# Decoder layer in split float32: one 512-column product in place of two of 256 columns

## The chip, the cores and the metric

One core of a Trainium2 chip runs the whole kernel. The metric is the device time of one execution in microseconds; of several executions the median is taken.

## What is computed

One hybrid decoder layer on 256 tokens of width 2048, in float32:

```python
h = rms_norm(x, attn_norm_g)
proj = h @ w_in                                   # 2048 x 4448
y_rwkv = rwkv7_mixer(token_shift(proj[...]), ...) # 16 heads of 64, a recurrence over the tokens
y_mla = mla_mixer(c_q, c_kv, k_pe, positions, ...)# 8 heads, latents of 512, causal softmax
x = x + concat(y_rwkv, y_mla) @ w_out
h = rms_norm(x, ffn_norm_g)
x = x + (silu(conv3(h @ w_gate)) * (h @ w_up)) @ w_down   # d_ff = 5632
return rms_norm(x, final_norm_g)
```

## The kernel before

All large products are made in three parts. A float32 factor is split into a high part (rounded to the matmul's input type) and a low part (the rest), and the product is hi·hi + hi·lo + lo·hi, all added in PSUM. Weights come from HBM in pieces of 128 x 1024 floats. `piece` (L118) loads one on SP's queue, ScalarE (ACT) rounds it into `hi` (L126) and VectorE (DVE) subtracts to get `lo` (L127). `raw`, `hi` and `lo` have three buffers each, so the cast for a piece needs the buffer that the piece three before it has left.

Two helpers issue the products. `prod_b` (L149) holds a weight tile of 128 x 128 in the array and streams the activations of all 256 tokens; the result is feature-major, 128 features x 256 tokens. For each tile of the contraction (a "k tile") it issues three matmuls of 256 columns: high weights with high activations (L160), high weights with low activations (L161), low weights with high activations (L162). Every matmul has a weight load of its own. `prod_a` (L165) holds activations and streams 512 columns of weights, also three matmuls per k tile and token block (L172 to L174); the change does not touch it.

`prod_b` serves three users:

- `in_tile` (L179): the 35 column tiles of the input projection, 16 k tiles each. The first five (three in `acc0`, two in `kacc`) are made while the kernel starts, before the row norms `rsB` are known; the first two go by L154 with `by_pass=True`: all four hi·hi, then all four hi·lo, then the lo·hi of a group of k tiles.
- `up_b` (L761): 10 pieces of the latents' up projection, two results of 4 k tiles each.
- the gated MLP (L914 to L935): 44 column tiles, gate and up, 16 k tiles each, in two blocks of 24 and 20; each block is followed by its part of the down projection, which is `prod_a`.

So there are 35·16 + 10·2·4 + 44·2·16 = 2048 k tiles in `prod_b`. A result occupies half of a PSUM bank tile of 128 x 512 (`mm`, three buffers). It is evicted by one VectorE multiplication with a per-token scale: `h` (L363, in `shifted`), `kraw` (L414), `cr` (L727), `dsts` (L767), `gt` (L924), `up` (L931).

The activations' two parts lie in separate tiles: `xhi`, `xlo` (two each, 8 k tiles per tile) for the input, `chi`, `clo` for the latents, `zhi`, `zlo` for the MLP. They are filled by a ScalarE operation and a VectorE subtraction each (L136, L137; L734, L735; L880, L881).

In time the stages are: start (to some 41 us), decay, keys, receptance, values with the triangular solves on VectorE beside them (to some 250 us), the recurrence over four chunks with the latents and `up_b` as matmuls between its steps (to some 349 us), attention and output projection (to some 490 us), MLP block 0, down, block 1, down. The order on each engine is not the program's: the tile framework places instructions by a simulated timeline (`schedule_with_timeline_sim=True`), SP's queue at the start by hand. Within one accumulator the matmuls stay in the program's order.

Of the kernel before, what the change touches and what calls it, by code (L numbers as in the profile page):

```python
# [17 lines left out]
P = 128  # L18
# [36 lines left out]
def hybrid_layer(ctx: ExitStack, tc: tile.TileContext, a: dict, out: bass.AP):  # L55
# [24 lines left out]

    def t1(n, w=T, dt=F32):
        return sb.tile([P, 260], dt, tag="t1", name=nm(n), bufs=NT1)[:, :w]
# [20 lines left out]
    xhi = [a8("xhi") for _ in range(2)]  # L103
    xlo = [a8("xlo") for _ in range(2)]
# [25 lines left out]
    def xsplit(g):  # L130
        raw = s4(n="xraw").rearrange("p (k t) -> p k t", k=4)
        nc.sync.dma_start(raw, xT[:, g * 4:(g + 1) * 4, :])
        for j in range(4):
            k = g * 4 + j
            h = xhi[k // 8][:, k % 8, :]
            S.activation(h, raw[:, j, :], AF.Copy, scale=vv("ag", k))  # L136
            V.scalar_tensor_tensor(xlo[k // 8][:, k % 8, :], raw[:, j, :], vv("ag", k),  # L137
                                   h.bitcast(F32), ALU.mult, ALU.subtract)
        return raw
# [36 lines left out]
    x_hi = lambda k: xhi[k // 8][:, k % 8, :]  # L176
    x_lo = lambda k: xlo[k // 8][:, k % 8, :]

    def in_tile(i, pf=mm):  # L179
        acc = pf()[:, :T]  # L180
        for h in range(2):
            prod_b(acc, piece(a["win"][i, h]), x_hi, x_lo, h * 8, 8, h == 0, h == 1)
            if h == 0:
                flush()
        return acc

    def rsqrt(src, scale, eps, w, eng=None, part=None):
        """1/sqrt(src * scale + eps) on [P, w]: integer seed and three Newton steps on -y."""
        e = eng or nc.gpsimd
        m, y, t = st("rm", w), st("ry", w), st("rt", w)  # L190
        if part is None:
            e.tensor_scalar(m, src, 0.5 * scale, 0.5 * eps, ALU.mult, ALU.add)
        else:
            e.tensor_scalar(part, part, 0.5 * scale, 0.5 * eps, ALU.mult, ALU.add)
# [24 lines left out]
    # sums over features of squares, token-major, accumulated over feature tiles  # L219
# [64 lines left out]
    # sigmoid(x) = 0.5 tanh(x/2) + 0.5  # L284
# [9 lines left out]
    acc0 = [mm()[:, :T], mm()[:, :T], at()[:, :T]]  # L294
# [11 lines left out]
    with tc.manual_schedule(engines={mybir.EngineType.SP}):  # L306
        for g in range(4):
            xsplit(g)
            if g == 0:
                nc.scalar.dma_start(cst, a["cst"])  # L310
            if g == 2:
                rope_tables()
            if g % 2 == 0:
                for i in range(2):
                    pcs[i, g // 2] = piece(a["win"][wt0[i], g // 2])
            for i in range(2):
                hl = tuple(u[:, (g % 2) * 512:(g % 2 + 1) * 512] for u in pcs[i, g // 2])
                prod_b(acc0[i], hl, x_hi, x_lo, g * 4, 4, g == 0, g == 3, True)
        for h in range(2):
            prod_b(acc0[2], piece(a["win"][26, h]), x_hi, x_lo, h * 8, 8, h == 0, h == 1)  # L320
# [93 lines left out]
    V.tensor_tensor(kraw[0:64], acc[0:64], rsB[0:64], ALU.mult)  # L414
# [36 lines left out]
    # squared inverse key norms: token-major [t, (p, w, h)], and per problem  # L451
# [266 lines left out]
    chi, clo, rrs, rrB = [], [], [], []  # L718

    def latent(x, gname, post):  # L720
        h_, l_ = s4(F32R, "chi"), s4(F32R, "clo")
        h_, l_ = (u.rearrange("p (k t) -> p k t", k=4) for u in (h_, l_))
        ssum = t2("css")
        for j in range(4):
            acc = in_tile(27 + x * 4 + j)
            cr = t2("cr")
            V.tensor_tensor(cr, acc, rsB, ALU.mult)  # L727
# [6 lines left out]
            S.activation(h_[:, j, :], cr, AF.Copy, scale=vv(gname, j))  # L734
            V.scalar_tensor_tensor(l_[:, j, :], cr, vv(gname, j), h_[:, j, :].bitcast(F32), ALU.mult, ALU.subtract)  # L735
# [11 lines left out]
        chi.append(h_)  # L747
        clo.append(l_)
# [12 lines left out]
    def up_b(src, i, x, dsts):  # L761
        pcs = piece(src[i])
        for j in range(2):
            acc = mm()[:, :T]
            prod_b(acc, (pcs[0][:, j * 512:(j + 1) * 512], pcs[1][:, j * 512:(j + 1) * 512]),
                   lambda k: chi[x][:, k, :], lambda k: clo[x][:, k, :], 0, 4, True, True)
            V.tensor_tensor(dsts[j], acc, rrB[x], ALU.mult)  # L767
# [24 lines left out]
    for cc in range(2):  # L792
        accs = [mm() for _ in range(2)]
        for i in range(2):
            prod_a(accs, piece(a["wuv"][cc, i]), lambda k: chi[1][:, k, :], lambda k: clo[1][:, k, :],
# [60 lines left out]
    zhi, zlo = zip(*((a8("zhi"), a8("zlo")) for _ in range(2)))  # L856
    for half in (0, 1):
        for c in range(4):
# [8 lines left out]
            if half == 1:  # L867
# [3 lines left out]
                for j in range(2):  # L871
# [5 lines left out]
                    for k in range(2):  # L877
                        kt = c * 4 + j * 2 + k
                        hv = zhi[kt // 8][:, kt % 8, :]
                        S.activation(hv, pt[:, k, :], AF.Copy, scale=vv("fg", kt))  # L880
                        V.scalar_tensor_tensor(zlo[kt // 8][:, kt % 8, :], pt[:, k, :], vv("fg", kt),  # L881
# [8 lines left out]
    z_hi = lambda k: zhi[k // 8][:, k % 8, :]  # L890
    z_lo = lambda k: zlo[k // 8][:, k % 8, :]
# [19 lines left out]
    for blk, nf in enumerate((24, 20)):  # L911
        hh = [s4(F32R, "hh").rearrange("p (k t) -> p k t", k=4) for _ in range(nf // 4)]
        hl = [s4(F32R, "hl").rearrange("p (k t) -> p k t", k=4) for _ in range(nf // 4)]
        for fi in range(nf):  # L914
            f = f0 + fi
            accs = []
            for gu in range(2):
                acc = mm()[:, :T]
                for h in range(2):
                    prod_b(acc, piece(a["wgu"][f, gu, h]), z_hi, z_lo, h * 8, 8, h == 0, h == 1)  # L920
# [3 lines left out]
            V.tensor_tensor(gt[:, 2:258], accs[0], rs2B, ALU.mult)  # L924
# [6 lines left out]
            V.tensor_tensor(up, accs[1], rs2B, ALU.mult)  # L931
# [117 lines left out]
```

## Time and profile before

| | |
|---|---|
| time, three runs | median 1246.21 us (1246.03 to 1254.26) |
| span of the profiled execution | 1248.2 us |
| TensorE (PE) busy | 1227.7 us, 98% |
| weight loads (PEld) | 1129.7 us, 91% |
| VectorE (DVE) busy | 786.2 us, 63% |
| ScalarE (ACT) busy | 563.9 us, 45% |
| granted clock of TensorE, mean | 0.992 |

The profiled execution is one execution, and its span is 2.0 us above the median of the timed runs. Matmuls are pipelined: one's duration in the trace (some 283 ns) overlaps the next, so a matmul's price in a dense stretch is the distance from one start to the next, not its duration.

### The profile page before, as it was taken

The page shows a single profiled execution, that of the slowest core. Times are in us where ns is not written, and L with a number is a line of the kernel's source. Part 1 is how long each engine was busy: PE and PEld are TensorE (multiplying, and loading weights), DVE is VectorE, ACT ScalarE, POOL GpSimd, SP SyncE. Part 2 cuts the span into 40 slices and gives each one's busy share as a digit, 9 for nine tenths or more (in the row PEclk, how much of TensorE's full clock was granted, in tenths as well). Part 3 has the DMA queues.
Part 4 walks back from the last instruction along what each step waited for, and adds up shares of the span by engine and source line. Part 5 has one row for each costly group of instructions (what it writes and reads, how often), then busy time and mean ns, then how long its engine had stood idle before and what let it go on. Part 6 is the DMA issues. An engine that isn't in the chain of part 4 may idle for free.

```text
span 1248.2 us, 22026 instructions
## 1 busy us (share of the span) xinstructions
PE 1227.7 (98%) x8945; PEld 1129.7 (91%) x8945; DVE 786.2 (63%) x1195; ACT 563.9 (45%) x787; POOL 52.3 (4%) x196
## 2 busy tenths in 40 slices
PE   7999999999999999999999999999999999999996
PEld 6889999998867888999999999888899999998885
DVE  6886658755667566666666665545466666665563
ACT  6773245422234445544444444333344444444451
POOL 3300000101110001000000000000000000000000
PEclk9999999998999999999999999999999999999999
DMA  8634445733323455565555555656655555566662
GB/s 305 197 120 141 124 147 178 201 114 114 111 85 128 159 178 176 176 183 183 186 185 181 181 183 186 193 188 191 201 187 186 181 180 184 184 218 205 213 205 87
DMA packets 70773, 216.04 MB, mean 173 GB/s; under 512 B 17360, under 2 KB 17616, under 8 KB 70672
## 3 DMA queue, kind: packets, MB, share of 16 engines
q1 hardware_dynamic: 69520, 211.84, 53.5%
q10 hardware_dynamic: 768, 2.05, 0.5%
q8 instruction: 70, 1.15, 0.4%
q0 software_dynamic: 384, 0.75, 0.2%
q14 instruction: 31, 0.25, 0.1%
HBM read 210.48 MB, written 3.41 MB: 171 GB/s over the span
## 4 chain that ended last, share of the span: by engine, by line
PE 97%; DMA 1%; DVE 1%; issue 0%; ACT 0%; ACTq 0%; POOL 0%; DVEq 0%; POOLq 0%
PE mm L160 19%; PE mm L162 19%; PE mm L161 19%; PE mm L172 9%; PE mm L173 9%; PE mm L174 9%; PE pg L504 1%; PE px L636 1%; PE px L645 1%; PE psc L816 1%; DMA raw<-in_win 1%; PE px L632 1%; PE py L662 1%; PE psc L814 1%; PE mm L154 0%; DMA rp<-in_pos 0%
## 5 line engine op out<-in xcount | busy, mean ns | idle before, releaser
L127 DVE TENSOR_TENSOR lo<-raw,hi 128x1024 fp32r<-128x1024 f32 x376 | 460.5, 1225 | 295.2 <-ACT hi L126 290.7
L126 ACT CAST hi<-raw 128x1024 fp32r<-128x1024 f32 x376 | 394.8, 1050 | 551.9 <-PE mm L161 222.5
L160 PE MATMUL mm<-zhi,hi 128*128 128x256 f32 x1408 | 398.3, 283 | 0.0
L162 PE MATMUL mm<-zhi,lo 128*128 128x256 f32 x1408 | 396.7, 282 | 0.0
L161 PE MATMUL mm<-zlo,hi 128*128 128x256 f32 x1408 | 396.3, 282 | 0.0
L161 PEld LDWEIGHTS mm<-zlo,hi 128*128 128x128 f32 x1408 | 266.1, 189 | 0.1
L162 PEld LDWEIGHTS mm<-zhi,lo 128*128 128x128 f32 x1408 | 265.5, 189 | 0.0
L160 PEld LDWEIGHTS mm<-zhi,hi 128*128 128x128 f32 x1408 | 263.8, 188 | 0.1
L160 PE MATMUL mm<-xhi,hi 128*128 128x256 f32 x496 | 143.1, 288 | 1.1 <-DVE h L363 1.1
L161 PE MATMUL mm<-xlo,hi 128*128 128x256 f32 x496 | 143.6, 289 | 0.0
L162 PE MATMUL mm<-xhi,lo 128*128 128x256 f32 x496 | 142.8, 288 | 0.2 <-DVE lo L127 0.2
L174 PE MATMUL mm<-hi,hl 128*128 128x512 f32 x336 | 130.9, 390 | 0.0
L173 PE MATMUL mm<-lo,hh 128*128 128x512 f32 x336 | 130.8, 389 | 0.0
L172 PE MATMUL mm<-hi,hh 128*128 128x512 f32 x336 | 119.5, 390 | 0.0
L161 PEld LDWEIGHTS mm<-xlo,hi 128*128 128x128 f32 x496 | 94.6, 191 | 3.2 <-issue 2.0
L162 PEld LDWEIGHTS mm<-xhi,lo 128*128 128x128 f32 x496 | 94.6, 191 | 2.7 <-issue 2.0
L160 PEld LDWEIGHTS mm<-xhi,hi 128*128 128x128 f32 x496 | 94.5, 191 | 2.7 <-ACT hi L126 1.2
L174 PEld LDWEIGHTS mm<-hi,hl 128*128 128x128 f32 x336 | 63.1, 188 | 13.2
L173 PEld LDWEIGHTS mm<-lo,hh 128*128 128x128 f32 x336 | 63.1, 188 | 13.0
L172 PEld LDWEIGHTS mm<-hi,hh 128*128 128x128 f32 x336 | 63.1, 188 | 13.0
L173 PE MATMUL mm<-lo,yhi 128*128 128x512 f32 x128 | 51.4, 401 | 0.0
L174 PE MATMUL mm<-hi,ylo 128*128 128x512 f32 x128 | 50.8, 397 | 0.0
(282 smaller groups left out, 1263.3 us busy)
## 6 DMA issues: line engine op xcount, KB each, us to landing
raw<-in_wgu SPq DMA_DIRECT2D x176, 512.0 KB, 3.5
raw<-in_wdn SPq DMA_DIRECT2D x88, 512.0 KB, 3.8
raw<-in_win SPq DMA_DIRECT2D x70, 512.0 KB, 3.5
raw<-in_wout SPq DMA_DIRECT2D x32, 512.0 KB, 3.6
raw<-in_wuq SPq DMA_DIRECT2D x6, 512.0 KB, 3.4
xraw<-in_xT SPq DMA_DIRECT2D x4, 512.0 KB, 6.2
xt<-in_x SPq DMA_DIRECT2D x4, 512.0 KB, 6.6
raw<-in_wuk SPq DMA_DIRECT2D x4, 512.0 KB, 3.7
```

What stands on the lines that cost most here:

```text
L126: S.copy(hi, raw)
L127: last_lo[0] = V.tensor_tensor(lo, raw, hi.bitcast(F32), ALU.subtract).ins
L160: PE.matmul(acc, wh, ah, start=first and j == 0, stop=False)
L161: PE.matmul(acc, wh, al, start=False, stop=False)
L162: PE.matmul(acc, wl, ah, start=False, stop=last and j == n - 1)
L172: PE.matmul(accs[tb], ah, wh, start=first and j == 0, stop=False)
L173: PE.matmul(accs[tb], ah, wl, start=False, stop=False)
L174: PE.matmul(accs[tb], al, wh, start=False, stop=last and j == n - 1)
L504: PE.matmul(pg[:, o:o + P], BK[pp][hs, gg, w, par * 2:par * 2 + 2, :], AR[pp][hs, gg, w * 2 + par, :, :], start=True, stop=True)
L632: PE.matmul(px[rs_, a_ * P:(a_ + 1) * P], AR[pp][:, g, c, 0, :], ST[hf][:, a_, :], start=True, stop=True)
L636: PE.matmul(px[rs_, e * 64:(e + 1) * 64], G1[c][hf][rs_, e, 0:64], UV[c][rs_, p, h * 64:h * 64 + 64], start=c == 0, stop=True, skip_group_ ...
L645: PE.matmul(pu[ru_, e * 64:(e + 1) * 64], TT[rs_, w * 16 + hf * 8 + e, :], xs[rs_, e * 64:(e + 1) * 64], start=True, stop=True, skip_group ...
```

## The change

The two parts of the activations are stored side by side, per k tile first 256 high columns and then 256 low ones (`hl4`, tiles `xs_`, `cl`, `zs`, as many bytes as before). `prod_b` issues one matmul of 512 columns (high weights with both parts) and one of 256 (low weights with the high part), the latter onto the first half of the same bank. The two halves are then added at eviction by the new `joined`. `by_pass` is gone. Every eviction of a `prod_b` result calls `joined`. `prod_a` reads the same values from the new places.

```diff
+    def hl4(n):
+        return a8(n).rearrange("p (k s) t -> p k s t", s=2)
...
-    xhi = [a8("xhi") for _ in range(2)]
-    xlo = [a8("xlo") for _ in range(2)]
+    xs_ = [hl4("x") for _ in range(4)]
...
-    def prod_b(acc, pieces, act_hi, act_lo, kt0, n, first, last, by_pass=False):
+    def prod_b(acc, pieces, act, kt0, n, first, last):
         hi, lo = pieces
-        if by_pass:
-            for q, (w, act) in enumerate(((hi, act_hi), (hi, act_lo), (lo, act_hi))):
-                for j in range(n):
-                    PE.matmul(acc, w[:, j * P:(j + 1) * P], act(kt0 + j), start=first and q + j == 0,
-                              stop=last and q == 2 and j == n - 1)
-            return
         for j in range(n):
-            ah, al = act_hi(kt0 + j), act_lo(kt0 + j)
-            wh, wl = hi[:, j * P:(j + 1) * P], lo[:, j * P:(j + 1) * P]
-            PE.matmul(acc, wh, ah, start=first and j == 0, stop=False)
-            PE.matmul(acc, wh, al, start=False, stop=False)
-            PE.matmul(acc, wl, ah, start=False, stop=last and j == n - 1)
+            ac = act(kt0 + j)
+            PE.matmul(acc, hi[:, j * P:(j + 1) * P], ac, start=first and j == 0, stop=False,
+                      skip_group_check=True)
+            PE.matmul(acc[:, :T], lo[:, j * P:(j + 1) * P], ac[:, 0, :], start=False,
+                      stop=last and j == n - 1, skip_group_check=True)
+    def joined(dst, acc, scale, rows=slice(0, P)):
+        S.copy(dst, acc[rows, T:])
+        V.tensor_tensor(dst, acc[rows, :T], dst, ALU.add)
+        V.tensor_tensor(dst, dst, scale[rows], ALU.mult)
...
-                prod_b(acc0[i], hl, x_hi, x_lo, g * 4, 4, g == 0, g == 3, True)
+                prod_b(acc0[i], hl, x_hl, g * 4, 4, g == 0, g == 3)
...
-        V.tensor_tensor(h[rows, 1:257], acc[rows], rsB[rows], ALU.mult)
+        joined(h[rows, 1:257], acc, rsB, rows)
...
-            V.tensor_tensor(gt[:, 2:258], accs[0], rs2B, ALU.mult)
+            joined(gt[:, 2:258], accs[0], rs2B)
...
-            V.tensor_tensor(up, accs[1], rs2B, ALU.mult)
+            joined(up, accs[1], rs2B)
```

## Rows read from the trace of the kernel before

**Rows 1.** The page's totals: busy time, share of the span, instructions, by engine.

```profile
span 1248.2 us, 22026 instructions
...
PE 1227.7 (98%) x8945; PEld 1129.7 (91%) x8945; DVE 786.2 (63%) x1195; ACT 563.9 (45%) x787; POOL 52.3 (4%) x196
```

**Rows 2.** The page's chain that ended last, shares of the span by line.

```profile
PE mm L160 19%; PE mm L162 19%; PE mm L161 19%; PE mm L172 9%; PE mm L173 9%; PE mm L174 9%; PE pg L504 1%; PE px L636 1%; PE px L645 1%; PE psc L816 1%; DMA raw<-in_win 1%; PE px L632 1%; PE py L662 1%; PE psc L814 1%; PE mm L154 0%; DMA rp<-in_pos 0%
```

**Rows 3.** Groups by line: shapes, count, busy us, mean ns, idle time before, its releaser.

```profile
L160 PE MATMUL mm<-zhi,hi 128*128 128x256 f32 x1408 | 398.3, 283 | 0.0
...
L160 PE MATMUL mm<-xhi,hi 128*128 128x256 f32 x496 | 143.1, 288 | 1.1 <-DVE h L363 1.1
```

**Rows 4.** Timeline, TensorE, MLP: start us, duration us; 99 matmul steps between the two.

```profile
599.89 0.29 PE L160 MATMUL mm<-zhi,hi 128*128 128x256 f32 x1
...
611.78 0.28 PE L160 MATMUL mm<-zhi,hi 128*128 128x256 f32 x1
```

**Rows 5.** Timeline, TensorE, down projection: 51 steps of 512 columns between the two.

```profile
780.30 0.39 PE L172 MATMUL mm<-hi,hh 128*128 128x512 f32 x1
...
791.86 0.39 PE L172 MATMUL mm<-hi,hh 128*128 128x512 f32 x1
```

**Rows 6.** Timeline, TensorE, where 512 columns are followed by 256 in one stream.

```profile
898.39 0.39 PE L174 MATMUL mm<-hi,hl 128*128 128x512 f32 x1
898.62 0.28 PE L160 MATMUL mm<-zhi,hi 128*128 128x256 f32 x1
```

**Rows 7.** Timeline, TensorE, keys stage: eight steps of 256 columns between the two.

```profile
72.14 0.42 PE L161 MATMUL mm<-xlo,hi 128*128 128x256 f32 x1
...
73.85 0.42 PE L160 MATMUL mm<-xhi,hi 128*128 128x256 f32 x1
```

**Rows 8.** Stages: stretch, length; busy us (instructions) by engine; granted clock, DMA share, GB/s.

```profile
41.00:94.00 53.00, 51.93 (x368) 45.40 (x367) 45.91 (x98) 40.37 (x71) 3.68 (x16) 0.97 0.43 139
...
187.00:250.00 63.00, 63.00 (x584) 62.87 (x583) 52.41 (x105) 32.53 (x50) 4.26 (x18) 1.00 0.63 190
250.00:349.00 99.00, 98.53 (x1093) 89.11 (x1090) 59.69 (x98) 26.94 (x37) 11.63 (x32) 0.95 0.35 111
```

**Rows 9.** The same view for the MLP's first block.

```profile
490.00:765.00 275.00, 275.00 (x2293) 274.93 (x2292) 179.15 (x249) 133.64 (x178) 6.10 (x40) 1.00 0.58 183
```

**Rows 10.** Groups by line: additions, evictions and PSUM reads of 256 columns.

```profile
L932 DVE TENSOR_TENSOR up<-up,cv 128x256 f32<-128x256 f32 x44 | 18.7, 426 | 5.0 <-ACT cv L929 0.5
...
L931 DVE TENSOR_TENSOR up<-mm,rs2B 128x256 f32<-128x256 f32 x44 | 18.7, 425 | 27.2 <-PE mm L162 27.2
...
L837 ACT CAST yhi<-po 128x256 fp32r<-128x256 f32 x8 | 3.0, 372 | 13.5 <-PE po L836 13.4
```

**Rows 11.** Timeline, start of the kernel, four instructions.

```profile
8.11 1.22 PE L154 MATMUL mm<-xhi,hi 128*128 128x256 f32 x4 [8.11 <-ACT hi L126]
...
9.13 1.05 PE L154 MATMUL mm<-xlo,hi 128*128 128x256 f32 x4
...
9.73 1.22 DVE L127 TENSOR_TENSOR lo<-raw,hi 128x1024 fp32r<-128x1024 f32 x1
...
11.00 1.22 PE L154 MATMUL mm<-xhi,lo 128*128 128x256 f32 x4 [0.81 <-DVE lo L127]
```

**Rows 12.** Chain by time around 41 us: start us, length us, what.

```profile
41.75 0.44 DVE h L363
...
42.33 0.36 PE mm L160
```

**Rows 13.** Waits over the span: total us, times, longest us.

```profile
ACT hi L126 <- PE mm L161: 222.5, 128, 8.6
...
DVE gt L924 <- PE mm L162: 29.4, 43, 2.6
```

**Rows 14.** Timeline, MLP: one piece's cast and subtraction.

```profile
609.74 1.05 ACT L126 CAST hi<-raw 128x1024 fp32r<-128x1024 f32 x1 [1.40 <-PE mm L161]
610.82 1.23 DVE L127 TENSOR_TENSOR lo<-raw,hi 128x1024 fp32r<-128x1024 f32 x1 [1.31 <-ACT hi L126]
```

More of the change, by code (lines that the diff above doesn't have):

```diff
@@ L134, in xsplit @@
             k = g * 4 + j
-            h = xhi[k // 8][:, k % 8, :]
+            h = xs_[g][:, j, 0, :]
             S.activation(h, raw[:, j, :], AF.Copy, scale=vv("ag", k))
-            V.scalar_tensor_tensor(xlo[k // 8][:, k % 8, :], raw[:, j, :], vv("ag", k),
+            V.scalar_tensor_tensor(xs_[g][:, j, 1, :], raw[:, j, :], vv("ag", k),
                                    h.bitcast(F32), ALU.mult, ALU.subtract)
@@ L174, in prod_a @@
                 PE.matmul(accs[tb], al, wh, start=False, stop=last and j == n - 1)
-    x_hi = lambda k: xhi[k // 8][:, k % 8, :]
-    x_lo = lambda k: xlo[k // 8][:, k % 8, :]
+    x_hl = lambda k: xs_[k // 4][:, k % 4, :, :]
     def in_tile(i, pf=mm):
-        acc = pf()[:, :T]
+        acc = pf()
         for h in range(2):
-            prod_b(acc, piece(a["win"][i, h]), x_hi, x_lo, h * 8, 8, h == 0, h == 1)
+            prod_b(acc, piece(a["win"][i, h]), x_hl, h * 8, 8, h == 0, h == 1)
             if h == 0:
@@ L293, in hybrid_layer @@
     S.activation(warm, ones[:, 0:2], AF.Sin)
-    acc0 = [mm()[:, :T], mm()[:, :T], at()[:, :T]]
+    acc0 = [mm(), mm(), at()]
     pcs = {}
@@ L317, in hybrid_layer @@
                 hl = tuple(u[:, (g % 2) * 512:(g % 2 + 1) * 512] for u in pcs[i, g // 2])
-                prod_b(acc0[i], hl, x_hi, x_lo, g * 4, 4, g == 0, g == 3, True)
+                prod_b(acc0[i], hl, x_hl, g * 4, 4, g == 0, g == 3)
         for h in range(2):
-            prod_b(acc0[2], piece(a["win"][26, h]), x_hi, x_lo, h * 8, 8, h == 0, h == 1)
+            prod_b(acc0[2], piece(a["win"][26, h]), x_hl, h * 8, 8, h == 0, h == 1)
         sums(0)
@@ L413, in hybrid_layer @@
     kraw, ksw = t1("kraw"), t1("ksw")
-    V.tensor_tensor(kraw[0:64], acc[0:64], rsB[0:64], ALU.mult)
+    joined(kraw[0:64], acc, rsB, slice(0, 64))
     shifted(acc, 26, rows=slice(64, 96), dst=sg2)
@@ L715, in hybrid_layer @@
         chunk(c)
-    chi, clo, rrs, rrB = [], [], [], []
+    cl, rrs, rrB = [], [], []
     def latent(x, gname, post):
-        h_, l_ = s4(F32R, "chi"), s4(F32R, "clo")
-        h_, l_ = (u.rearrange("p (k t) -> p k t", k=4) for u in (h_, l_))
+        c_ = [s4(F32R, "cl").rearrange("p (k s t) -> p k s t", k=2, s=2) for _ in range(2)]
         ssum = t2("css")
@@ L726, in latent @@
             cr = t2("cr")
-            V.tensor_tensor(cr, acc, rsB, ALU.mult)
+            joined(cr, acc, rsB)
             if j == 0:
@@ L733, in latent @@
                 V.tensor_tensor(ssum, ssum, sq, ALU.add)
-            S.activation(h_[:, j, :], cr, AF.Copy, scale=vv(gname, j))
-            V.scalar_tensor_tensor(l_[:, j, :], cr, vv(gname, j), h_[:, j, :].bitcast(F32), ALU.mult, ALU.subtract)
+            h_, l_ = (c_[j // 2][:, j % 2, q, :] for q in range(2))
+            S.activation(h_, cr, AF.Copy, scale=vv(gname, j))
+            V.scalar_tensor_tensor(l_, cr, vv(gname, j), h_.bitcast(F32), ALU.mult, ALU.subtract)
         pss = at("pss")
@@ L746, in latent @@
         rrB.append(rb)
-        chi.append(h_)
-        clo.append(l_)
+        cl.append(c_)
     latent(0, "qg", SC)
@@ L763, in up_b @@
         for j in range(2):
-            acc = mm()[:, :T]
+            acc = mm()
             prod_b(acc, (pcs[0][:, j * 512:(j + 1) * 512], pcs[1][:, j * 512:(j + 1) * 512]),
-                   lambda k: chi[x][:, k, :], lambda k: clo[x][:, k, :], 0, 4, True, True)
-            V.tensor_tensor(dsts[j], acc, rrB[x], ALU.mult)
+                   lambda k: cl[x][k // 2][:, k % 2, :, :], 0, 4, True, True)
+            joined(dsts[j], acc, rrB[x])
     for i in range(4, 6):
@@ L794, in hybrid_layer @@
         for i in range(2):
-            prod_a(accs, piece(a["wuv"][cc, i]), lambda k: chi[1][:, k, :], lambda k: clo[1][:, k, :],
+            prod_a(accs, piece(a["wuv"][cc, i]), lambda k: cl[1][k // 2][:, k % 2, 0, :],
+                   lambda k: cl[1][k // 2][:, k % 2, 1, :],
                    i * 2, 2, i == 0, i == 1)
@@ L855, in hybrid_layer @@
     ssf = st("ssf", 8)
-    zhi, zlo = zip(*((a8("zhi"), a8("zlo")) for _ in range(2)))
+    zs = [hl4("z") for _ in range(4)]
     for half in (0, 1):
@@ L878, in hybrid_layer @@
                         kt = c * 4 + j * 2 + k
-                        hv = zhi[kt // 8][:, kt % 8, :]
+                        hv = zs[c][:, j * 2 + k, 0, :]
                         S.activation(hv, pt[:, k, :], AF.Copy, scale=vv("fg", kt))
-                        V.scalar_tensor_tensor(zlo[kt // 8][:, kt % 8, :], pt[:, k, :], vv("fg", kt),
+                        V.scalar_tensor_tensor(zs[c][:, j * 2 + k, 1, :], pt[:, k, :], vv("fg", kt),
                                                hv.bitcast(F32), ALU.mult, ALU.subtract)
@@ L887, in hybrid_layer @@
     bcast(rsqrt(ss2, 1.0 / DM, EPS, 2), rs2B)
-    z_hi = lambda k: zhi[k // 8][:, k % 8, :]
-    z_lo = lambda k: zlo[k // 8][:, k % 8, :]
+    z_hl = lambda k: zs[k // 4][:, k % 4, :, :]
     fgb = [None, None]
@@ L917, in hybrid_layer @@
             for gu in range(2):
-                acc = mm()[:, :T]
+                acc = mm()
                 for h in range(2):
-                    prod_b(acc, piece(a["wgu"][f, gu, h]), z_hi, z_lo, h * 8, 8, h == 0, h == 1)
+                    prod_b(acc, piece(a["wgu"][f, gu, h]), z_hl, h * 8, 8, h == 0, h == 1)
                 accs.append(acc)
```

## The prediction

> **What bounds the kernel now.** I read the page's totals first: PE is busy in 98% of the span, VectorE (DVE) in 63%, ScalarE (ACT) in 45% [rows 1]. A busy PE of overlapping matmuls need not be a bound, so the chain of waits comes next: three lines of `prod_b` hold 19% each, the three of `prod_a` 9% each, and one DMA and no other engine reaches 1% [rows 2]. The third view is the timeline of PE, which gives the price of one matmul as the distance between starts. In the MLP 99 steps of 256 columns take 611.78 − 599.89 = 11.89 us, 120.1 ns each [rows 4]. In the down projection 51 steps of 512 columns take 11.56 us, 226.7 ns each [rows 5]. The two differ by 106.6 ns for 256 columns, which is 2.4 GHz, and the granted clock of the MLP stage is 1.00 [rows 9]. So 256 columns cost 106.7 ns and 13.4 ns come on top; for 512 it is 213.3 and again 13.4. The groups show no idle time before the MLP's matmuls and 1.1 us before those of the input [rows 3]. The kernel is a stream of matmuls that waits for almost nothing, and each pays about 13.4 ns that do not depend on its length.
>
> **What the change removes.** Each k tile had three matmuls of 256 columns, 3 × 120.1 = 360.3 ns. It gets one of 512 and one of 256: 226.7 + 120.1 = 346.8. The columns are the same 768; one fixed part, 13.4 ns, goes. The two kinds do follow one another in the trace: a 256 comes 0.23 us after a 512, the same as 512 after 512 [rows 6]. By stage:
> - MLP: 1408 k tiles [rows 3] × 13.4 ns = 18.9 us. Nothing stands between the matmuls there, so I take all of it.
> - `in_tile` after the start: 30 tiles × 16 = 480 × 13.4 = 6.4 us, and `up_b`: 80 × 13.4 = 1.1 us.
> - the five tiles made at the start: 80 × 13.4 = 1.1 us at most; they run as their weights get cast, so I take 0.
>
> Together 26.4 us, at most 27.5. Where the clock is at 1.2 GHz a step is 1.71 / 8 = 0.214 us, which is 256 columns and no rest [rows 7]: such k tiles gain nothing. The mean clock is 0.97 in 41 to 94 us and 0.95 in 250 to 349 us [rows 8], so some 3 and 10 us run at half speed, a few per cent of the k tiles there; under 0.4 us, left out.
>
> The Trainium skill, page "TensorE: Matmul & The Clock Gate", section "Back-to-back issue gap", has a rule that speaks against the change: a matmul's gap at full clock is its columns at 2.4 GHz plus about 2.5 ns. By that figure the change would remove 1968 × 2.5 = 4.9 us in place of 26.4. The trace does not agree (13.4 ns at both lengths, where each matmul has a weight load of its own), so the sum goes by the rows.
>
> **What it adds at eviction.** `joined` makes three operations of one: a copy of half a bank on ACT, an addition on DVE, and the multiplication that was there, now from SBUF. A PSUM read of 256 columns costs 372 ns on ACT, an addition or multiplication 425 or 426 ns on DVE, from PSUM or SBUF alike [rows 10]. For 144 evictions that is 54 us on ACT and 61 us on DVE, all beside PE. In the MLP's first block (48 evictions) DVE rises from 179 us to 200 in about 265, ACT from 134 to 152 [rows 9]: neither is near full. What the addition could delay is the weights. There the cover is the triple buffering: the cast at 609.74 starts as PE leaves a piece, and the subtraction ends at 610.82 + 1.23 = 612.05 [rows 14]; the buffer is needed two pieces after PE left the first, 2 × 24 × 120.1 ns = 5.76 us, at about 615.4. That leaves 3.3 us. One eviction puts at most 0.37 us into ACT's queue and 0.43 into DVE's between two pieces. Cost 0. Without that cover every eviction would cost about 0.8 us. The bank is held 0.8 us longer; the next but one accumulator needs it, a whole tile of 5.5 us later. Cost 0.
>
> **What moves at the start.** `by_pass` let PE do eight matmuls before it needed the first low weights: two groups of four from 8.11 to 11.00 us, where it waited for `lo` [rows 11]. Now an accumulator takes one matmul of 512 columns and then needs `lo`. Before 11.00 us PE can do two of 512 (one per accumulator), the work of four, and four of 256 columns are left over: 4 × 0.12 = 0.5 us at full clock. PE also reaches 2.4 GHz later if it rests before 11.00: it ran 8.11 to 11.00, and if all 2.9 us of that shift behind, half speed costs up to 1.5 us more: 0.5 to 2.0 in all; I take the middle, 1.3, as no row shows that clock step alone.
>
> **A wait that goes.** At 41.75 us the first eviction multiplies by `rsB` and only then leaves its bank; PE's next tile starts at 42.33 [rows 12], and the groups put 1.1 us of PE's idle time to that `h` [rows 3]. In `joined` the copy and the addition do not need `rsB`; only the last step does, and it reads SBUF. The bank is free long before. Gain 0 to 1.1, I take 1.1, since nothing else that PE needs there hangs on `rsB`.
>
> **Recurrence.** From 250 to 349 us matmuls of latents and `up_b` fill the gaps of a chain over chunks. Their share of the gain is (128 + 80) × 13.4 = 2.8 us. If the chain sets the end of the stage, none of it is kept; if PE does (98.53 of 99 us busy [rows 8]), all. I take half: +1.4.
>
> **Sum.** −26.4 + 1.3 − 1.1 + 1.4 = −24.8 us. Against the profiled span of 1248.2 this gives 1223.4. The median of the timed runs is 2.0 us below that span, so the forecast is 1221.4 us, −2.0%. With the best ends (−27.5 + 0.5 − 1.1 = −28.1) it is 1218.1; I put the low end at 1216 for half-speed time that a denser stream may save in the recurrence.
>
> **Rivals.**
> - *DVE becomes the bound in the mixer.* It is busy 45.9 of 53 us in the keys stage and 52.4 of 63 beside the solves [rows 8]. Some 12 and 11 evictions add 12 × 0.426 = 5.1 and 4.7 us, which takes it to 96% and 91%. If all that and the recurrence's other 1.4 us end on the path: −24.8 + 11.2 = −13.6, 1232.6 us. For it: dependent work, the keys and the solves, sits in the same queue as the subtractions. Against: PE shows no wait for `lo` in these stages' groups beyond 1.1 us [rows 3].
> - *The fixed part is not saved*: the rest belongs to the columns streamed or to a change of weights, and a pair costs the 360.3 ns of three. Then the change only adds: 1.3 − 1.1 + 1.4 = +1.6, 1247.8 us. Against: 256 and 512 columns have the same rest [rows 4, 5], and the one mixed step read, 0.23 us, has it too [rows 6]. The rule of the Trainium skill cited above ("TensorE: Matmul & The Clock Gate", "Back-to-back issue gap") lies close to this case, with 4.9 us less: 1242.9 us.
> - *Slower: the copy blocks the casts on ACT.* The copy waits for PE's last matmul of its tile; casts queued behind it wait too. If the planner puts it one piece early, the cast that follows starts at that piece's end, and 0.37 + 1.05 + 1.23 = 2.65 us later `lo` is ready, just within the next piece of 8 × 346.8 ns = 2.77 us: no loss. If it puts it two pieces early, PE stalls 2.65 us per eviction; with the MLP's 88, 233 us come on top of −24.8: 1454 us. It decides from 10 such evictions on (24.8 / 2.65 = 9.4). Against: today's evictions wait for PE at DVE's head 29.4 us in 43 times, 0.7 us each, longest 2.6 [rows 13], so the planner places them a fraction of a piece early, and ACT waits 222.5 us for free buffers [rows 13], that is, it runs ahead as far as it may.
>
> **How the numbers follow.** Forecast 0.79, DVE rival 0.12, no fixed part saved 0.04, ACT rival 0.05. The range reaches from 1216 to 1235: the forecast's bounds and the DVE rival. The other two rivals, 0.09, lie above it, and some 0.1 is left for errors in the bounds. Within 1% (12.5 us) a measurement of this kernel cannot tell a change. The DVE rival ends near that line (1233.7), so its chance splits 0.07 to 0.05: faster 0.86, same 0.05 + 0.04 = 0.09, slower 0.05.
>
> **What would show it.** Right: in the MLP the pair's pitch is 0.347 us, 16 pairs take 5.55 us and the stage from first to last matmul of a block is shorter by 1.34 us per 100 k tiles; PE has two matmuls per k tile, with no idle time before them; the gap at 41 us is gone; DVE's busy time is some 60 us more, ACT's 54. Wrong: idle time before `prod_b`'s matmuls put to `lo` L127 or to the copy; a pitch of 0.36 us per pair; PE at half clock in stages where it was at 1.00; a recurrence stage as long as before.

## The result and the profile after

The changed kernel takes 1238.41 us (median of six runs, one disturbed run at 4508.89 us left out of the ratio) beside 1248.6 us for six runs of the kernel before on the same chip: ratio 0.9911, 95% interval 0.9883 to 0.994. It is 0.9% faster, where 2.0% were forecast, and lies above the range's upper end of 1235. Between the profiled spans the change is 1238.5 − 1248.2 = −9.7 us instead of −24.8.

The page of the kernel after: totals, the chain that ended last by line, and two groups (L157 is the matmul of 512 columns, L159 that of 256). They answer to [rows 1 to 3].

```profile
span 1238.5 us, 18227 instructions
...
PE 1206.4 (97%) x6897; PEld 1014.8 (82%) x6897; DVE 833.1 (67%) x1339; ACT 600.1 (48%) x931; POOL 56.6 (5%) x196
...
PE mm L157 37%; PE mm L159 19%; PE mm L177 9%; PE mm L176 9%; PE mm L178 9%; PE pg L507 1%; PE px L639 1%; DVE lo L130 1%; PE px L648 1%; PE psc L819 1%; PE px L635 1%; PE py L665 1%; PE psc L817 1%; DMA raw<-in_win 1%; DMA cst<-in_cst 1%
...
L157 PE MATMUL mm<-z,hi 128*128 128x512 f32 x1408 | 493.5, 393 | 0.3 <-ACT hi L129 0.3
...
L157 PE MATMUL mm<-x,hi 128*128 128x512 f32 x528 | 195.7, 408 | 16.7 <-DVE h L165 8.5
```

PE is still 97% busy and still the chain. But the matmuls of the input projection now have 16.7 us of idle time before them. Of these, 8.2 us are the wait at the very start, which stood with L154 before (8.1 us [rows 11]); 8.5 us are put to the addition in `joined` (L165), where the eviction L363 had 1.1 us [rows 3]. PE's busy time fell by 21.3 us, the span by 9.7.

I cut the span at marks that both traces have. The first matmul on `z` starts at 490.10 us before and 493.31 after: the work ahead of the MLP is 3.2 us longer. Block 0 of the MLP, first to last matmul start, takes 277.8 us before (490.10 to 767.89) and 271.7 after (493.31 to 765.02); block 1 takes 230.28 (898.62 to 1128.9) and 223.89 (895.74 to 1119.63). So the MLP gave 12.5 us, the part before it took back 3.2, and the down projections and the end make the other 0.4. Against the forecast, 6.4 us are missing in the MLP (18.9 − 12.5) and 9.1 ahead of it (5.9 forecast as a gain, 3.2 lost).

The MLP's price, timeline of PE after (start us, duration us); 35 pairs lie between the first and the last line. It answers to [rows 4].

```profile
599.59 0.39 PE L157 MATMUL mm<-z,hi 128*128 128x512 f32 x1
599.82 0.28 PE L159 MATMUL mm<-z,lo 128*128 128x256 f32 x1
599.94 0.39 PE L157 MATMUL mm<-z,hi 128*128 128x512 f32 x1
...
611.84 0.39 PE L157 MATMUL mm<-z,hi 128*128 128x512 f32 x1
```

A pair costs 12.25 / 35 = 350.0 ns, 233 of it after the 512-column matmul, 117 after the other. The forecast had 346.8. Against 360.0 for three it saves 10.0 ns per k tile. In block 1 that is all: 640 k tiles × 10.0 = 6.4 us. In block 0, 768 × 10.0 = 7.7, of which one late piece takes 1.5 us (steps of 0.60 and 1.26 us at 508.57 in place of 0.117 and 0.233; the second line waits for ACT's cast, the third for DVE's subtraction):

```profile
508.57 0.28 PE L159 MATMUL mm<-z,lo 128*128 128x256 f32 x1
509.17 0.49 PE L157 MATMUL mm<-z,hi 128*128 128x512 f32 x1 [0.32 <-ACT hi L129]
510.43 0.38 PE L159 MATMUL mm<-z,lo 128*128 128x256 f32 x1 [0.77 <-DVE lo L130]
```

Ahead of the MLP the first 42 us went a little better than forecast. The timeline of PE after: the start, where PE waits for the first low weights, and the tile that follows the first eviction (before: 42.33 [rows 12], now 41.42).

```profile
8.24 0.80 PE L157 MATMUL mm<-x,hi 128*128 128x512 f32 x1 [8.24 <-ACT hi L129]
11.26 0.58 PE L159 MATMUL mm<-x,lo 128*128 128x256 f32 x1 [2.22 <-DVE lo L130]
...
41.42 0.47 PE L157 MATMUL mm<-x,hi 128*128 128x512 f32 x1
```

At 41.4 us the changed kernel is 0.9 us ahead, where the forecast had it 0.2 behind: the wait of 1.1 us went, and the start cost 0.2 us net of what its k tiles saved, not 1.3. The largest loss comes in one place. PE, ACT and DVE after, 175 to 184 us; L548 is the first operation of the triangular solves (its operand `Lp` comes back from HBM by DMA), L164 and L165 are `joined`'s copy and addition:

```profile
175.69 0.28 PE L159 MATMUL mm<-x,lo 128*128 128x256 f32 x1
...
177.10 0.38 ACT L164 COPY h<-mm 128x256 f32<-128x256 f32 x1
182.00 1.23 DVE L548 TENSOR_TENSOR Lp<-Lp,Mp 128x1024 f32<-128x1024 f32 x1 [3.82 <-DMA Lp<-dL]
...
183.66 0.42 DVE L165 TENSOR_TENSOR h<-mm,h 128x256 f32<-128x256 f32 x1
...
184.13 0.79 PE L157 MATMUL mm<-x,hi 128*128 128x512 f32 x1 [7.95 <-DVE h L165]
```

The copy has read its half of the bank at 177.48. The addition that frees the bank stands in DVE's queue behind L548, which waits 3.82 us for the DMA. All three `mm` banks hold finished tiles (the first three values tiles, whose last matmuls end at 156.2, 164.8 and 176.0), so PE rests 7.95 us, and up to 188.5 its clock is at the lower level: 256 columns take some 0.21 us. The kernel before has the same order in DVE's queue, at nearly the same time (L545 is the solves' first operation, L363 the eviction):

```profile
181.03 1.23 DVE L545 TENSOR_TENSOR Lp<-Lp,Mp 128x1024 f32<-128x1024 f32 x1 [0.62 <-DMA Lp<-dL]
182.36 0.19 DVE L549 TENSOR_TENSOR tm<-Tq,Lp 128x31 f32<-128x31 f32 x1
182.47 0.42 DVE L363 TENSOR_TENSOR h<-mm,rsB 128x256 f32<-128x256 f32 x1
```

There the first values tile stands behind L545 too, but PE still had work: its third values tile ends with the first line below, and the next one takes the freed bank with the second.

```profile
183.67 0.28 PE L162 MATMUL mm<-xhi,lo 128*128 128x256 f32 x1
183.79 0.28 PE L160 MATMUL mm<-xhi,hi 128*128 128x256 f32 x1
```

The eviction had freed that bank at 182.47 + 0.42 = 182.89, so PE could have come 0.9 us earlier and no more. It comes 183.67 − 175.69 = 8.0 us earlier (3.6 of them saved in `prod_b`, 1.1 the wait that went, the rest shorter steps of other matmuls, not explained), and the bank is free 1.2 us later, at 184.08.

Stretches of PE, before and after (stretch, length, busy us of PE, PEld, DVE, ACT, POOL, granted clock, DMA share, GB/s):

```profile
160.00:200.00 40.00, 40.00 (x327) 38.83 (x327) 28.45 (x57) 19.33 (x30) 0.59 (x6) 1.00 0.52 167
345.00:400.00 55.00, 55.00 (x273) 37.25 (x273) 39.13 (x63) 22.57 (x48) 5.00 (x14) 1.00 0.33 105
```

```profile
160.00:200.00 40.00, 32.05 (x180) 27.08 (x180) 25.41 (x57) 15.17 (x27) 0.40 (x4) 0.87 0.40 113
345.00:400.00 55.00, 53.09 (x243) 35.13 (x242) 36.06 (x57) 20.97 (x43) 7.25 (x15) 0.88 0.24 76
```

The second stretch holds a smaller case: scores wait 1.55 us at 379.87 for an exponential behind DVE's group norm, and again PE goes on at the lower clock.

What PE's time ahead of the MLP was spent on, as the sum of distances from each matmul's start to the next one's start (us; a wait counts to the matmul in front of it). The last two columns are experiments 9 and 10 below.

| matmuls | before | after | before, no solves | after, no solves |
|---|---|---|---|---|
| `prod_b` | 250.7 | 243.3 | 251.4 | 244.3 |
| `prod_a` | 102.6 | 104.3 | 101.6 | 101.9 |
| all others | 128.7 | 137.5 | 130.8 | 122.5 |
| sum | 482.0 | 485.1 | 483.8 | 468.7 |

`prod_b` itself became 7.4 us shorter (640 k tiles at 10.0 ns would be 6.4; the rest was not taken apart). The other matmuls, to which the 7.95 us wait counts, became 8.8 us longer.

### The profile page after: what moved, and what is told of

The parts are those of the page before. It is cut to its first block, busy times and chain, and to the rows that moved or that the text cites. A ratio compares the mean times of both kernels' runs of the same rounds, so it can differ in the third digit from the quotient of the medians.

```text
span 1238.5 us, 18227 instructions
## 1 busy us (share of the span) xinstructions
PE 1206.4 (97%) x6897; PEld 1014.8 (82%) x6897; DVE 833.1 (67%) x1339; ACT 600.1 (48%) x931; POOL 56.6 (5%) x196
## 4 chain that ended last, share of the span: by engine, by line
PE 93%; DVE 3%; DMA 2%; ACT 1%; issue 1%; POOL 1%; ACTq 0%; SPq 0%; DVEq 0%
PE mm L157 37%; PE mm L159 19%; PE mm L177 9%; PE mm L176 9%; PE mm L178 9%; PE pg L507 1%; PE px L639 1%; DVE lo L130 1%; PE px L648 1%; PE psc L819 1%; PE px L635 1%; PE py L665 1%; PE psc L817 1%; DMA raw<-in_win 1%; DMA cst<-in_cst 1%
## 5 line engine op out<-in xcount | busy, mean ns | idle before, releaser
L157 PE MATMUL mm<-z,hi 128*128 128x512 f32 x1408 | 493.5, 393 | 0.3 <-ACT hi L129 0.3
L159 PE MATMUL mm<-z,lo 128*128 128x256 f32 x1408 | 393.1, 279 | 0.8 <-DVE lo L130 0.8
L157 PEld LDWEIGHTS mm<-z,hi 128*128 128x128 f32 x1408 | 263.8, 187 | 63.4 <-ACT hi L129 0.6
L159 PEld LDWEIGHTS mm<-z,lo 128*128 128x128 f32 x1408 | 263.8, 187 | 1.2 <-DVE lo L130 1.1
L157 PE MATMUL mm<-x,hi 128*128 128x512 f32 x528 | 195.7, 408 | 16.7 <-DVE h L165 8.5
L159 PE MATMUL mm<-x,lo 128*128 128x256 f32 x528 | 153.8, 291 | 2.2 <-DVE lo L130 2.2
L157 PEld LDWEIGHTS mm<-x,hi 128*128 128x128 f32 x528 | 102.3, 194 | 41.0 <-ACT hi L129 8.2
L159 PEld LDWEIGHTS mm<-x,lo 128*128 128x128 f32 x528 | 102.3, 194 | 5.4 <-DVE lo L130 2.7
L176 PE MATMUL mm<-hi,yhi 128*128 128x512 f32 x128 | 49.8, 403 | 0.0
L157 PE MATMUL mm<-cl,hi 128*128 128x512 f32 x80 | 29.6, 408 | 0.0
```

The source lines that it names most:

```text
L157: PE.matmul(acc, hi[:, j * P:(j + 1) * P], ac, start=first and j == 0, stop=False, skip_group_check=True)
L159: PE.matmul(acc[:, :T], lo[:, j * P:(j + 1) * P], ac[:, 0, :], start=False, stop=last and j == n - 1, skip_group_check=True)
L176: PE.matmul(accs[tb], ah, wh, start=first and j == 0, stop=False)
```

## The experiments

All ratios are against runs of the kernel before on the same chip, with 95% intervals.

**1 and 2. The change in halves.** The first has the pair and `joined` in the MLP alone, the second everywhere but in the MLP.

```diff
--- the kernel before; 1: prod_p makes the pair, the rest as before
-prod_b(acc, piece(a["wgu"][f, gu, h]), z_hi, z_lo, h * 8, 8, h == 0, h == 1)
+prod_p(acc, piece(a["wgu"][f, gu, h]), z_hl, h * 8, 8, h == 0, h == 1)
...
-V.tensor_tensor(up, accs[1], rs2B, ALU.mult)
+joined(up, accs[1], rs2B)
--- the kernel after; 2: prod_t makes three of 256 columns
-prod_b(acc, piece(a["wgu"][f, gu, h]), z_hl, h * 8, 8, h == 0, h == 1)
+prod_t(acc, piece(a["wgu"][f, gu, h]), z_hl, h * 8, 8, h == 0, h == 1)
...
-joined(up, accs[1], rs2B)
+V.tensor_tensor(up, accs[1], rs2B, ALU.mult)
```

> The pair of one 512 and one 256 column matmul, the activations side by side and the joined eviction in the gated MLP alone; input projection and latents as before. Theory A (the pair is worth 10 ns per k tile in place of 13.4, and the 9 us that are missing besides were lost before the MLP): the MLP's two blocks, 277.8 and 230.3 us before, take 270 to 272 and 223.9 us; the stretch ahead of the MLP is as before, 490 us; the span is about 1234 to 1236, 1 to 1.2% under the kernel before and some 3 us under the whole change. Rival B (the evictions cost PE time wherever they are): the blocks gain less than 6 us together.

> The pair and the joined eviction in everything ahead of the MLP alone; the MLP with three matmuls of 256 columns and one multiplication per eviction, as before. Theory A: the MLP starts at 493 us in place of 490, its blocks take 277.8 and 230.3 us, the span is about 1251, 0.2% over the kernel before. Rival (what was lost ahead of the MLP is an accident of one execution): the MLP starts at 484 us or earlier and the span is 1242 or less.

Measured: MLP alone 1237.75 us, 0.9904 (0.9883 to 0.9926); all but the MLP 1250.88 us, 1.0019 (1.0 to 1.0038), with the MLP's start at 494.31. The MLP alone makes the whole gain, and the other half gives nothing where 5.9 us were forecast. Nor does it cost anything clear of the scatter: experiment 1 was expected 3 us under the whole change and is 0.7 under it. In experiment 1, which has the old input projection, the MLP begins at 492.15 us (490.10 in the kernel before): some 2 us of such a mark are scatter, and experiment 4 shows more.

**3. Evictions without the saving.** After, but the matmul of high weights split into two of 256 columns: three matmuls per k tile as before, with `joined`.

```diff
-PE.matmul(acc, hi[:, j * P:(j + 1) * P], ac, start=first and j == 0, stop=False,
+wh = hi[:, j * P:(j + 1) * P]
+PE.matmul(acc[:, :T], wh, ac[:, 0, :], start=first and j == 0, stop=False, skip_group_check=True)
+PE.matmul(acc[:, T:], wh, ac[:, 1, :], start=False, stop=False, skip_group_check=True)
```

> The whole change but for the matmuls: three of 256 columns per k tile again, high and low halves kept apart in the bank, joined at eviction. It has the added eviction work without the matmuls' gain. Theory A (the gain is in the matmuls' fixed part, the loss in the order of work ahead of the MLP): the MLP's steps are 120.1 ns again, its blocks 278 and 230 us, and the stretch ahead of the MLP is longer than before by 3 to 10 us: span 1251 to 1258. Rival (evictions are hidden everywhere and the loss came with the faster matmuls): 490 us ahead of the MLP, span 1248.

Measured: 1251.19 us, 1.0021 (1.0006 to 1.0035). The MLP's blocks take 278.0 and 230.28 us: `joined` costs nothing there. Its MLP begins at 493.17, and that of the kernel after at 493.31. Experiment 2 differs from this run ahead of the MLP by the pair (and the planner's order with it), and its median is only 0.3 us less (1250.88): ahead of the MLP the shorter matmuls bought nothing. After its first matmul PE rests 4.7 us there with three matmuls and 13.3 with the pair (2.5 before). At the solves, PE's wait is 2.7 us with three matmuls and 7.95 with the pair: the evictions make the smaller part of it, PE's earlier arrival the larger.

**4. Where the 256 columns go.** The low weights' matmul adds onto the second half of the bank instead of the first.

```diff
-PE.matmul(acc[:, :T], lo[:, j * P:(j + 1) * P], ac[:, 0, :], start=False,
+PE.matmul(acc[:, T:], lo[:, j * P:(j + 1) * P], ac[:, 0, :], start=False,
```

> The whole change, with the low weights' product added onto the second half of the bank in place of the first; the sum at eviction is the same. If the 6 ns that a 256 column matmul starts later after a 512 column one come from adding onto the columns that the 512 wrote first, the step changes from 232 to 227 ns or to more than 232 and the MLP's blocks move by 4 us or more. If they belong to the change of length, the pair stays at 350 ns and the span within 2 us of the whole change's 1238.

Measured: 1240.83 us, 0.9917 (0.9888 to 0.9946), pair 350 ns. The half of the bank does not set the price. The run also shows the scatter of the part ahead of the MLP: PE's and DVE's order there is that of the kernel after, and its MLP begins at 497.67 us, 4.4 later. Experiment 7 has the same order too and begins it at 487.94, so that order alone spreads over 10 us. The granted clock is what differs (240 to 270 us of after, experiment 4 and experiment 7; the clock is the third number from the end):

```profile
240.00:270.00 30.00, 30.00 (x428) 26.73 (x426) 17.88 (x30) 8.50 (x14) 3.83 (x14) 0.94 0.49 141
240.00:270.00 30.00, 30.00 (x370) 26.95 (x369) 16.22 (x27) 6.47 (x11) 3.83 (x14) 0.77 0.47 122
240.00:270.00 30.00, 30.00 (x437) 26.62 (x437) 19.41 (x34) 9.66 (x16) 3.83 (x14) 1.00 0.43 134
```

Differences of a few us between two such marks therefore show little; the ratios of several runs show more.

**5 and 6. The solves later in DVE's queue.** `pend.append(solve)` moves from before the values loop into it, after the first or the second values tile.

```diff
-    pend.append(solve)
...
             vt.append(shifted(in_tile(17 + pp * 2 + g), 17 + pp * 2 + g))
+            if pp == 0 and g == 0:      # experiment 6: g == 1
+                pend.append(solve)
```

> The whole change; the triangular solves are handed to the planner one column tile later, so that the eviction of the first value tile stands ahead of the solves' first instruction (the one that waits for a DMA) in VectorE's queue. Theory A (8 us of PE idle at 176 us come from three accumulators that stand unevicted behind that waiting instruction): PE runs one tile more, 5.6 us, the idle time shrinks to 2 to 3 us and the half-clock stretch behind it goes; if PE binds afterwards the MLP starts 5 to 8 us earlier, at 486 to 488, and the span is about 1232. Rival C (a chain through the solves and the recurrence, not PE, sets the end of the stretch): the idle time shrinks as said, but the MLP starts at 492 to 495 as before and the span stays at 1237 to 1240.

> As the run before, one tile later still: two value tiles are evicted ahead of the solves. Theory A: no idle time at 176 us; the MLP starts at 484 to 488. Rival C: the solves start later or at the same time, the chain moves with them, and the MLP starts at 493 us or later.

Measured: 1237.84 us, 0.9893 (0.9876 to 0.9909), and 1235.67 us, 0.987 (0.9854 to 0.9887). The MLP begins at 490.80 and 488.04. In experiment 6 DVE evicts two more tiles before it meets the solves' first operation at 181.18, and PE has no wait left there (windows, 160 to 250 us, of after and of experiment 6: PE's busy time is the second number):

```profile
160.00:250.00 90.00, 82.05 (x576) 71.07 (x576) 68.54 (x143) 43.08 (x74) 0.53 (x6) 0.94 0.56 166
```

```profile
160.00:250.00 90.00, 88.96 (x524) 77.03 (x523) 70.78 (x146) 48.73 (x80) 4.80 (x18) 1.00 0.62 179
```

In this stretch PE gets 6.9 us back, and the clock. The MLP's start is 5.3 us earlier than in the kernel after, which lies within the spread of such marks (487.94 in experiment 7 without the move); by the ratios the gain on the kernel after is some 5 us (0.987 and 0.9911, whose intervals just meet). This order is the best complete version of this study. By the ratio it is 16.3 us under the kernel before (14.1 to 18.3); without the MLP's 12.5 some 2 to 6 us are left ahead of it, an estimate from two numbers. Experiment 5 lies between its two expectations, with 4.4 us of the wait left, and experiment 6 at the edge of theory A. What is next behind the wait these runs do not settle.

**7. What a matmul of 512 columns costs in the MLP.** Column tiles take turns: three of 256, the pair with 256 first, two of 512 (which adds low times low), the pair.

```diff
+steps = (((z, wh, ac[:, 0, :]), (z, wl, ac[:, 0, :]), (slice(T, 2 * T), wh, ac[:, 1, :])),
+         ((z, wl, ac[:, 0, :]), (slice(0, 2 * T), wh, ac)),
+         ((slice(0, 2 * T), wh, ac), (slice(0, 2 * T), wl, ac)),
+         ((slice(0, 2 * T), wh, ac), (z, wl, ac[:, 0, :])))[form]
```

> The whole change, with four forms of a k tile in the MLP by column tile: (0) three of 256 columns whose weights change each time (high, low, high); (1) the pair with the 256 first; (2) two of 512 columns, the low weights' product of the low parts being added as well; (3) the pair as it is. If a repeated weight tile makes the following matmul's fixed part smaller (the three of the kernel before used the high weights twice in a row), form 0 costs about 365 to 370 ns against 360 before and form 2 about 457. If the change of length is what costs 3 ns, form 0 is 360, form 2 is 453.4 = 2 x 226.7, forms 1 and 3 are 350.

Measured, ns per k tile: 360.0, 350.3, 466.6, 350.3. Two of 512, timeline of PE, 56 steps between the two lines:

```profile
612.39 0.39 PE L174 MATMUL mm<-z,hi 128*128 128x512 f32 x1
...
625.46 0.39 PE L174 MATMUL mm<-z,hi 128*128 128x512 f32 x1
```

13.07 / 56 = 233.4 ns. Nothing changes length here, so the 6.6 ns over the down projection's 226.7 [rows 5] are not the price of a change from 512 to 256: the 512 columns themselves cost more in this place. The trace of the kernel before shows the same outside the down projection. Its output projection, full clock, the same helper as the down projection, 15 steps between the two lines:

```profile
464.49 0.40 PE L172 MATMUL mm<-hi,yhi 128*128 128x512 f32 x1
...
468.00 0.39 PE L172 MATMUL mm<-hi,yhi 128*128 128x512 f32 x1
```

3.51 / 15 = 234.0 ns. I had read one stage's price and taken it for the chip's.

**8. PE made shorter ahead of the MLP by leaving work out.** The kernel before without the low-weights matmul in the input projection from tile 3 on.

```diff
-PE.matmul(acc, wl, ah, start=False, stop=last and j == n - 1)
+if not skip_low:
+    PE.matmul(acc, wl, ah, start=False, stop=last and j == n - 1)
```

> The kernel before, with the matmuls of the low weights left out in 32 of the 35 column tiles of the input projection (512 matmuls of 120 ns, 61 us of PE; weights are still loaded and split, and the projection lacks its lo x hi part). It asks how much of PE time that is taken out ahead of the MLP comes back. If PE binds there, as the prediction took it, the MLP starts 56 to 62 us earlier, at 430. Rival C (chains bind a part of it): it starts less than 40 us earlier, with PE idle or at half clock for the rest.

Measured: 1237.83 us, 0.9888 (0.9868 to 0.9907). Some 512 matmuls of 120 ns went, 61 us of PE, for 13.9 us: the MLP begins at 476.21. PE rests 36.7 us ahead of it (2.5 before). Windows, and the waits of two lines (total us, times, longest us):

```profile
160.00:250.00 90.00, 68.36 (x637) 67.06 (x638) 65.17 (x128) 39.81 (x59) 6.36 (x19) 0.82 0.57 172
```

```profile
PE pR L594 <- DMA T<-dU: 10.9, 1, 10.9
PE mm L160 <- DVE h L364: 9.9, 2, 8.8
```

`pR` is the first matmul of the recurrence, and `T` the solves' result on its way back through HBM. Of the 47 us that did not come back, 34 are rests of PE (36.7 − 2.5); the trace also has 61.4 us at half clock ahead of the MLP, where the kernel before has 13.6. So something else sets the end once PE is 14 us shorter, and what PE waits for are DVE's evictions and the chain of Gram matrices, HBM, solves on DVE, HBM, `pR`.

**9 and 10. Without the solves.** The solves' loop of 31 steps is left out, of the kernel before and of the kernel after; the copies and DMAs around it stay.

```diff
-        for i in range(31):
+        for i in range(0):
```

> The kernel before without the 31 steps of the triangular solves (the loads and stores around them stay; the recurrence gets unit matrices). The chain on VectorE from the solves' first instruction to the copy of their result, 57 us from 181 to 238 before, shrinks to a few us. Theory C (ahead of the MLP the time is set by that chain and the work behind it, with PE's stream only just filling it): the MLP starts 3 to 10 us earlier than 490, as PE has little idle time to give back there. Rival (PE alone binds): less than 3 us.

> The whole change without the 31 steps of the solves. Theory C: with the chain gone the matmuls' gain comes through, and the MLP starts at least 4 us earlier than in the kernel before without its solves (560 to 640 k tiles x 10 ns = 5.6 to 6.4 us), where with the solves it starts 3.2 us later than before. Rival D (the added evictions cost more than the matmuls gain, chain or not): it starts no earlier than the kernel before without its solves.

Measured: before without solves 1251.62 us, 1.0017 (0.9996 to 1.0037), no difference; after without solves 1226.44 us, 0.9823 (0.9797 to 0.985). Totals of the two pages:

```profile
span 1249.8 us, 21974 instructions
...
PE 1225.9 (98%) x8945; PEld 1128.9 (90%) x8945; DVE 767.4 (61%) x1133; ACT 563.9 (45%) x787; POOL 55.3 (4%) x196
```

```profile
span 1222.0 us, 18165 instructions
...
PE 1199.7 (98%) x6897; PEld 1009.9 (83%) x6897; DVE 815.7 (67%) x1277; ACT 600.3 (49%) x931; POOL 57.0 (5%) x196
```

In the kernel before the solves cost nothing, against the expectation of 3 to 10 us: PE covers them. In the kernel after they cost 12 us. Not all of that is the solves' length: in experiment 10 DVE also evicts the first three values tiles (155.86, 164.25, 175.62) ahead of the solves' first operation (180.12), as experiment 6 does with two. By the ratios of after, 6 and 10 (0.9911, 0.987, 0.9823) about half of the 12 us is that order and half the solves, an estimate. Between the two kernels without solves the change is worth 25.2 us by the medians and 27.8 by the profiled spans, 15.0 of the latter ahead of the MLP (491.78 to 476.82). The table above takes these 15.0 apart: `prod_b` 7.1 us, and the other matmuls 8.2, more than the forecast had; with another order on every engine, which waits and half-speed stretches make up the 8.2 is not settled.

**11. Which matmuls of 512 columns cost 226.7.** Four forms of two, by column tile: results onto two banks in turn; weights taken from the activations; activations as weights and weights as moving data, as in `prod_a`; both onto one bank (as in experiment 7). Only the first and the last compute the product.

```diff
+steps = (((acc, wh, ac), (acc2, wl, ac)),
+         ((acc, z0, ac), (acc, z1, ac)),
+         ((acc, z0, hi[:, c]), (acc, z1, lo[:, c])),
+         ((acc, wh, ac), (acc, wl, ac)))[form]
```

> The whole change, with four forms of two 512 column matmuls per k tile in the MLP by column tile (of these only (0) and (3) compute the products): (0) high and low weights into two banks by turns; (1) both weight tiles taken from the activations, which nothing writes at that time; (2) activations as weights and the weight pieces streamed, the roles that they have in the down projection; (3) high and low weights into one bank. The down projection's step is 226.7 ns, form (3) was 233.3. If turns of banks matter, (0) is 226.7; if it is weights that come from freshly split pieces, (1) and (2) are 226.7; if it is the activations as the streamed operand, (2) alone is 226.7.

Measured, median step of a form's column tiles: 233.5, 227.3, 234.2, 233.3 ns. The timeline of the second form (42 alike in one line, 9.68 us with the last one's 0.39: 9.29 / 41 = 226.6 ns) and of the last (36 steps, 8.40 / 36 = 233.3):

```profile
633.70 9.68 PE L175 MATMUL mm<-z 128*128 128x512 f32 x42
...
664.21 0.39 PE L175 MATMUL mm<-z,hi 128*128 128x512 f32 x1
...
672.61 0.39 PE L175 MATMUL mm<-z,hi 128*128 128x512 f32 x1
```

Neither the bank nor the roles decide. The second form, which reads no fresh weights, reaches 226.6 after some eight steps of 224 to 236. What it shares with the down projection stays open.

**12. The multiplication on GpSimd.** Experiment 6, with the last step of `joined` moved off DVE for the input tiles from 9 on and the latents.

```diff
-        V.tensor_tensor(dst, dst, scale[rows], ALU.mult)
+        (nc.gpsimd if pool else V).tensor_tensor(dst, dst, scale[rows], ALU.mult)
```

> The run with the solves handed over two tiles later, and besides the last multiplication of the joined eviction done by GpSimd for the receptance, value and latent tiles, so that VectorE has one operation of 0.42 us less for each of 24 tiles around the solves. If VectorE's load stretches the solves' chain (Lp to the copy of Tq, 58 us in that run), it shrinks by 3 to 5 us and the MLP starts at 484 to 486 us, span 1229 to 1231. If GpSimd's operation is slow or gets in VectorE's way, the chain is as long or longer and the span 1233 or more.

Measured: 1236.22 us, 0.9916 (0.9884 to 0.9948); MLP at 489.25. The solves' chain on DVE, from `Lp` to the copy of the result, became 2.4 us shorter (181.6 to 237.0 instead of 181.2 to 239.0), but nothing was gained over experiment 6: GpSimd takes 736 ns for what takes DVE 420, and what reads the result waits longer. Lightening DVE's queue by this much is not enough.

## Why the prediction was wrong, step by step

- **The MLP's term, 18.9 us at 13.4 ns per k tile: mechanism right, size wrong.** It gave 12.5. A pair costs 350.0 ns, not 346.8, so a k tile saves 10.0 ns (14.1 us for 1408), and 1.5 us went in the one late piece. The failing step is "226.7 + 120.1": 226.7 was the down projection's price, while the output projection of the same trace has 234.0. The mixed step that I called the same, 0.23 us [rows 6], has two digits and could not tell 226.7 from 233. Read from both stages, the saving had been 6 to 13 ns. The 2.5 ns that the prediction takes from the Trainium skill (page "TensorE: Matmul & The Clock Gate", section "Back-to-back issue gap") stand there for the gap of an isolated matmul; the section says that a stream of weight loads and matmuls, as here, is spaced otherwise, and the prediction left this condition out. By that figure the MLP would have saved some 2.5 ns per k tile; the trace does not agree, 10.0 were measured.
- **The input projection and `up_b`, 7.5 us less 1.3 at the start: came on PE, and then was lost.** `prod_b` ahead of the MLP is 7.4 us shorter; that this meets the 7.5 is partly luck, since a k tile saved 10.0 ns and not 13.4. The wait for `rsB` went as said; the start's term, 1.3 us, was too large (0.9 us ahead at 41.4 where 0.2 behind follows from the sum).
- **"The bank is held 0.8 us longer … Cost 0": the step that failed.** It gave `joined`'s addition its own duration and no place in a queue. The bank's tile was finished at 156.2; the copy read it from 177.10, and the addition freed it only at 184.08, because it stood behind an operation that waited for a DMA. The three banks were full by then. The single multiplication of the kernel before stood in the same place, and its bank was free 0.9 us before PE needed it: that was all the slack there was, and neither this step nor the saving taken in full for the input projection looked for it. Experiments 5 and 6, which hand the solves over one and two tiles later, take the wait away in part and wholly.
- **"The kernel is a stream of matmuls that waits for almost nothing": true of before, and no ground for the sum.** It says who is last, not how far the next one is behind. Experiment 8 shows that even without longer evictions 61 us less of PE give 14; experiments 2 and 3 that the shorter matmuls give nothing ahead of the MLP once `joined` is there; experiments 9 and 10 that the solves, with their place in DVE's queue, are what it collides with. Without them the gain is of the forecast's size (25.2 us), but by other terms, so by luck: 12.5 in the MLP where 18.9 were forecast, 15.0 ahead of it where 5.9 were. The half that I kept for the recurrence (+1.4) was of this kind, far too small, and one stage too late: PE waits from 176 us on.
- **The DVE rival had the place and not the form.** It looked for a busy DVE: 96% in the keys stage and 91% beside the solves. What it held against that, no wait for `lo` beyond 1.1 us, reads a row of waits for `h` [rows 3]. DVE is 49 of 53 us busy in the keys stage and between 160 and 250 us no busier than before (69.1 and 68.5 us). What stopped PE was the order in DVE's queue at one point. Its time (1232.6) came out 6 us too low, since it kept the MLP's 18.9.
- **Cost 0 of the evictions in the MLP: right** (experiment 3: 278.0 and 230.28 us). **The rival of ACT's copy: did not happen**; the one stall of 1.5 us is far from 2.65 per eviction. **No fixed part saved: did not happen either**, 10.0 ns of 13.4 were.

## What to carry to other kernels

When the bound engine gets shorter, ask how far behind it the next chain is, and read that from the slack of the buffers between them (here a bank freed at 182.89 and taken at 183.79) and from what stands at the head of the other engines' queues; busy shares do not show it. An eviction in several steps frees its bank when its last PSUM read gets its turn in a queue, not when its durations add up. Read the price of a shape in every stage that has it, with as many steps as give the digit that the sum needs.

## What was not expected of the hardware

A step of 512 columns at full clock, a weight load with each, costs 226.7 ns in the down projection and in one form of experiment 11, and 232 to 234 ns in the output projection, the input projection and the MLP; 256 columns cost 120 ns among themselves and 117 to 118 behind 512. Which bank, which half, which roles and whether lengths change made no difference. After a rest of 8 us, and after one of 1.6 us, PE went on at half clock; these two stretches make 24.0 of the 30.7 us at half clock ahead of the MLP, where the kernel before has 13.6. A rest does not always bring it: in experiment 9 PE rests 2.13 us at 349.25 and goes on at full clock.
